# A hybrid decoder layer: PSUM tiles, ScalarE reads, gathered diagonal blocks, and two Z projections moved into the attention steps

## The chip, the cores and the metric

The kernel runs on one core of a Trainium2 chip. The metric is the device time of one execution in microseconds (us); several runs of a kernel are taken, and their median counts. The engines are TensorE (PE; its weight loads are listed as PEld), VectorE (DVE), ScalarE (ACT), GpSimd (POOL) and SyncE (SP, which here only issues DMAs). Each works through its own instructions in order.

## The reference, cut to what matters

One decoder layer on x of 1024 tokens by 1024 channels, float32:

```python
h = rmsnorm(x, attn_norm_w)
qkv_la, z_la, b_la, a_la, q_d, k_d, v_d = split(h @ w_in)
q, k, v = split(silu(causal_conv(qkv_la)))
o_la = rmsnorm(gated_delta_rule(q, k, v, g, beta)) * silu(z_la)
o_d = rmsnorm(diff_attention(q_d, k_d, v_d, lam, bias))
x = x + concat(o_la, o_d) @ w_out
gate, up = split(rmsnorm(x) @ w_gate_up)
x = x + (silu(gate) * up) @ w_down
return rmsnorm(x)
```

The delta rule works in chunks of 64 tokens and needs, per head and chunk, the solution of a unit lower triangular system. The attention has four heads with two softmax maps each, causal, in blocks of 128 queries. z_la has four heads of 128 columns; head h of it multiplies the normed output of the delta rule's head h and is needed nowhere before.

## The kernel before, in words

Every float32 matrix product is made of three matmuls (`mm3`, lines 143 to 146): both operands are split into a rounded part (`_h`) and a rest (`_l`), and h·h, h·l and l·h are added up in PSUM. `split` (148) makes the two parts of a weight: a cast on ScalarE (151), and a subtraction on VectorE (153) or, in two halves, on GpSimd (157). Projections keep the transposed input `xT_h`, `xT_l` in SBUF and take 48 matmuls of 512 columns per 128 output columns (8 slices of the depth, 2 halves of the tokens, 3 matmuls).

PSUM is used through three names: `big` (two tiles of two banks, 1024 columns), `sm` and `fl` (two tiles of one bank each). Instructions are put in order by a planner which goes by the program order, by what each one waits for, and by a cost of its own; only the SP queue is kept in the written order from the attention on (`manual_schedule`, 1024).

The stages in order:

- Norm and transposition of x, the projection of v_d and of the gates (to line 296), and small tables.
- Conv stage (463 to 486): for each of four heads the projections of k and q (`dense_T`, 415), the convolution and Silu, the sums of squares, and the products k·k and k·q, which give `At` (482, the triangular matrices, 128 x 128 each) and `intra` (485, in place in `dec`). Behind it two powers on GpSimd (489, 490) and the scaling of `rqs` on VectorE (491); rqs is used after the scan only (702).
- Triangular solve (498 to 515): the 32 x 32 diagonal blocks of all At are transposed into `B` by four transposes of 32 partitions each (504), inverted by 31 steps of two VectorE instructions (509, 511), and transposed back (514, 515). Meanwhile TensorE makes the attention's q and k projections of heads 0 and 1 (`qk_dense`, 517; called at 558) and two conv projections of v. `qk_dense` reads each half (512 columns) from PSUM twice for these heads: ScalarE writes the rounded part (535), VectorE the rest (536); then ScalarE's queue issues the stores (544, 545 for q, 547, 548 for k).
- The block inverses are put together (lines 585 to 624), the keys transposed (625), and the remaining v projections made.
- The scan over 8 chunk pairs (653 to 701), with Z projections between its small matmuls; then the rest of the four Z projections (709 to 713): a projection into a `big` tile, one Silu of 1024 columns on ScalarE, a store to `sz_dr`. The weights' rests come from VectorE.
- Attention: 32 steps (head, block of queries). `emit_S` (908) makes the scores, VectorE adds the bias and takes the maximum (932 to 938), ScalarE the exponential (942), `emit_P` VectorE's combination of the two maps (951 to 954), `emit_T` the transposition (969), `emit_PV` the product with V (984). Between these parts `pump` takes matmuls out of a generator `fill` (807): the q and k projections of heads 2 and 3, the gating of the delta rule's output (`finish_norm`, `finish_gate`, which loads sz_dr), and the output projection (`out_unit`, 787, with w_out's weights from `fetch_o`). `share` (886) says how many matmuls a step takes: 22 - 5i/2 for block i, less what other calls take. `fetch` (398) issues a weight load on SP, `take` (404) splits it. `load_head` (722) loads a head's q, k and bias.
- Norm and transposition again (to 1137), then 22 turns of gate and up (`gate_up`, 1215). A turn computes two products of 256 x 256 blocks of tokens and depth halves with seven block products instead of eight: `product` (1197), 12 matmuls each, seven per turn. `banks` (1203) gives four PSUM tiles: pa from `sm`, pb from `fl`, and pc and pd as the two halves of one `big` tile. VectorE's additions (`add`, 1213) read them. Turn 0 is written out (1289 to 1321).
- The down projection and the last norm (1350 to 1397).

## Time and profile before

| | us |
|---|---|
| three runs, median | 1364.12 (1363.31 to 1366.2) |
| the profiled execution's own time | 1363.61 |
| its span, first to last instruction | 1361.5 |
| mean granted TensorE clock | 0.99 of full speed |

The rows further down are lines of this one profiled execution. Times in them count from its first instruction. A line of a timeline or of the chain begins with the start and the duration in us. "L536" is line 536 of the kernel; "[6.28 <-DVE cv L536]" says that the engine stood idle for 6.28 us before, until VectorE's instruction of line 536 on tile cv was done. Names of tiles are those of the program, with buffer numbers left out, so `av` or `cv` stands for several arrays.

### The profile page before, as it was taken

To read this page: it belongs to the slowest core of one execution; us is meant where nothing else is said; L and a number is where in the kernel's file an instruction comes from. 1 tells how busy PE (TensorE), PEld (TensorE's weight loads), DVE (VectorE), ACT (ScalarE), POOL (GpSimd) and SP (SyncE) were. 2 spreads that over 40 slices of the span, in tenths; PEclk is the share of its full clock that TensorE was granted. 3 is DMA by queue.
4 is the path that set the end of the run, shared out by engine and by line. 5 is a ranking of instruction groups with operands and counts; after the bars stand their busy time and mean duration, and the time that the engine had idled before them with its cause. 6 is when DMAs were issued, how large, how long until landed. Compare 5 with 4: busy or idle time off the path is not lost.

```text
span 1361.5 us, 16980 instructions
## 1 busy us (share of the span) xinstructions
PE 1298.3 (95%) x6540; PEld 1078.0 (79%) x6540; DVE 766.1 (56%) x1286; ACT 484.7 (36%) x920; POOL 240.6 (18%) x195
## 2 busy tenths in 40 slices
PE   6999998899999998989889999999999999999997
PEld 6978886798988777877668777878787888888886
DVE  6515659634836675876875465545544546545325
ACT  5233321132725564654543332322332234112104
POOL 1010030200023331232321212121122114200003
PEclk9999998999999998999989999999999999999999
DMA  7321112301146466735322323222222147422003
GB/s 218 111 62 43 35 32 88 114 17 31 33 141 196 144 206 183 227 102 200 119 78 93 108 82 104 87 70 77 93 78 92 63 156 276 140 93 93 0 1 124
DMA packets 122424, 143.30 MB, mean 105 GB/s; under 512 B 13632, under 2 KB 90728, under 8 KB 122344
## 3 DMA queue, kind: packets, MB, share of 16 engines
q1 hardware_dynamic: 114432, 128.07, 30.1%
q10 hardware_dynamic: 7912, 14.16, 2.8%
q8 instruction: 51, 0.84, 0.2%
q14 instruction: 29, 0.24, 0.1%
HBM read 103.40 MB, written 38.80 MB: 104 GB/s over the span
## 4 chain that ended last, share of the span: by engine, by line
PE 72%; DVE 12%; DMA 5%; issue 4%; ACT 4%; POOL 2%; SPq 1%; POOLq 0%; DVEq 0%; ACTq 0%
PE big L1200 17%; PE sm L1200 8%; PE big L144 4%; PE big L146 4%; PE big L145 4%; PE fl L144 4%; PE fl L146 4%; PE fl L145 4%; PE fl L1200 4%; PE sm L144 3%; PE sm L145 3%; PE sm L146 3%; PE sm L984 1%; DVE tmp L509 1%; DVE av L511 1%
## 5 line engine op out<-in xcount | busy, mean ns | idle before, releaser
L144 PE MATMUL big<-xT_h,w_h 128*128 128x512 f32 x320 | 128.2, 401 | 10.7 <-DVE cv L536 10.0
L146 PE MATMUL big<-xT_h,w_l 128*128 128x512 f32 x320 | 126.5, 395 | 0.0
L145 PE MATMUL big<-xT_l,w_h 128*128 128x512 f32 x320 | 126.1, 394 | 0.0
L1213 DVE TENSOR_TENSOR av<-big,av 128x512 f32<-128x512 f32 x88 | 60.5, 689 | 107.9 <-PE big L1200 107.8
L1200 PE MATMUL big<-hT_h,cv 128*128 128x512 f32 x264 | 90.8, 405 | 2.3 <-DVE av L1213 2.3
L1200 PE MATMUL big<-hT_h,avl 128*128 128x512 f32 x264 | 89.3, 399 | 1.2 <-DVE av L1213 1.2
L144 PEld LDWEIGHTS big<-xT_h,w_h 128*128 128x128 f32 x320 | 60.6, 190 | 26.0 <-DVE cv L536 12.3
L151 ACT CAST w_h<-w_raw 128x1024 fp32r<-128x1024 f32 x32 | 33.5, 1052 | 124.6 <-PE big L145 103.2
L146 PEld LDWEIGHTS big<-xT_h,w_l 128*128 128x128 f32 x320 | 60.5, 189 | 13.1 <-DVE w_l L153 0.7
L145 PEld LDWEIGHTS big<-xT_l,w_h 128*128 128x128 f32 x320 | 60.6, 189 | 11.8 <-issue 0.2
L1200 PEld LDWEIGHTS big<-hT_h,cv 128*128 128x128 f32 x264 | 50.4, 191 | 20.2 <-DVE av L1213 9.8
L1200 PEld LDWEIGHTS big<-hT_h,avl 128*128 128x128 f32 x264 | 49.5, 188 | 18.3 <-DVE av L1213 8.1
L1200 PE MATMUL sm<-hB_h,avl 128*128 128x512 f32 x176 | 59.0, 397 | 1.1 <-ACT hB_h L1130 1.1
L157 POOL TENSOR_TENSOR w_l<-w_raw,w_h 128x512 fp32r<-128x512 f32 x28 | 37.8, 1371 | 124.5 <-ACT w_h L151 123.3
L1213 DVE TENSOR_TENSOR x<-fl,x 128x512 f32<-128x512 f32 x48 | 32.9, 686 | 46.1 <-PE fl L146 46.1
L1213 DVE TENSOR_TENSOR x<-sm,x 128x512 f32<-128x512 f32 x48 | 33.0, 687 | 44.9 <-PE sm L146 44.1
L1200 PE MATMUL sm<-hB_h,cv 128*128 128x512 f32 x176 | 57.9, 389 | 0.0
L1168 DVE TENSOR_TENSOR xh<-w_raw 128x512 f32<-128x512 f32 x45 | 31.0, 688 | 46.8 <-DMA w_raw<-in_w_gate_up 46.8
L942 ACT ACTIVATE ae<-big,mx 128x128 f32<-128x128 f32 (+7 forms) x64 | 47.3, 741 | 27.9 <-DVE mx L933 11.8
L1105 POOL TENSOR_TENSOR avl<-xh,avl 128x512 fp32r<-128x512 f32 x23 | 30.7, 1335 | 148.4 <-ACT avl L1104 148.4
L1105 POOL TENSOR_TENSOR cv<-xh,cv 128x512 fp32r<-128x512 f32 x22 | 28.4, 1289 | 146.7 <-ACT cv L1104 146.7
L1200 PE MATMUL big<-hT_l,cv 128*128 128x512 f32 x132 | 52.6, 398 | 0.0
(431 smaller groups left out, 3480.8 us busy)
## 6 DMA issues: line engine op xcount, KB each, us to landing
w_raw<-in_w_gate_up SPq DMA_DIRECT2D x44, 512.0 KB, 4.0
w_raw<-in_w_in SPq DMA_DIRECT2D x24, 512.0 KB, 4.0
act<-av SPq DMA_DIRECT2D x22, 512.0 KB, 2.6
w_raw<-act SPq DMA_DIRECT2D x22, 512.0 KB, 4.3
cv<-in_w_down SPq DMA_DIRECT2D x20, 512.0 KB, 4.0
xt<-in_x SPq DMA_DIRECT2D x8, 512.0 KB, 5.1
ks<-cv ACTq DMA_DIRECT2D x8, 512.0 KB, 13.7
aqh<-qh SPq DMA_DIRECT2D x16, 256.0 KB, 5.6
```

Source lines behind the costliest of these rows:

```text
L144: nc.tensor.matmul(ps, lhsT=lh, rhs=rh, start=start, stop=False)
L145: nc.tensor.matmul(ps, lhsT=lh, rhs=rl, start=False, stop=False)
L146: nc.tensor.matmul(ps, lhsT=ll, rhs=rh, start=False, stop=stop)
L151: nc.scalar.copy(out=h, in_=raw)
L157: eng.tensor_tensor(out=l[:, c], in0=raw[:, c], in1=h[:, c].bitcast(F32), op=ALU.subtract)
L509: nc.vector.tensor_tensor(out=tv, in0=B[:, i + 1:, i:i + 1].broadcast_to([P, nr, ncol]), in1=X[:, i:i + 1, :ncol].broadcast_to([P, nr, nco ...
L511: nc.vector.tensor_tensor(out=X[:, i + 1:, :ncol], in0=X[:, i + 1:, :ncol], in1=tv, op=ALU.subtract)
L942: nc.scalar.activation(out=e[:, :n].rearrange("p (b c) -> p b c", b=nb), in_=s[:, :, :w], func=AF.Exp, bias=mx[:, m:m + 1], accum_out=zs[: ...
L1105: eng.tensor_tensor(out=l, in0=raw, in1=h.bitcast(F32), op=ALU.subtract)
L1168: nc.vector.tensor_tensor(out=r, in0=a0, in1=a1, op=alu)
L1200: nc.tensor.matmul(ps, lhsT=x[:, k, :], rhs=y[:, k, :], start=begin and k == 0 and n == 0, stop=k == HALF - 1 and n == 2, skip_group_check ...
L1213: nc.vector.tensor_tensor(out=out, in0=in0, in1=in1, op=ALU.add)
```

## The change

Five edits:

1. `banks` takes two `big` tiles per turn and uses the first half of each; turn 0 keeps the two halves of one.
2. `qk_dense` of heads 0 and 1 reads PSUM with ScalarE twice, the second time as the full value into `sl`; VectorE subtracts the rounded part once for both halves, from SBUF.
3. In the conv stage ScalarE copies the diagonal blocks of each new At into an array `diag` (32 copies of 32 partitions x 4 x 32), and one transpose over 128 partitions makes `B`.
4. The scaling of rqs moves behind the assembly of the inverses.
5. Z projections 2 and 3 leave the loop behind the scan. They become the first part of `fill` (`z_dense`), with `fl` tiles, a Silu per half, and the weights' rests on GpSimd; their weights are fetched ahead of head 0's q and k, the weight loads for q and k of head 2 follow behind them, and the shares rise to 24.67 - 5i/2.

```diff
@@ -460,6 +460,7 @@
             nc.vector.tensor_reduce(out=dst[:, hh, half * 4:half * 4 + 4],
                                     in_=ps.rearrange("p (a b) -> p a b", a=4), axis=AX.X, op=ALU.add)
 
+    diag = op.tile([P, T], F32, name="av", bufs=4).rearrange("p (h c) -> p h c", c=32)
     for h in range(H):
         conv_silu(dense_T(C_K + h * P), 4 + h, KT[h])
         conv_silu(dense_T(C_Q + h * P), h, QT[h])
@@ -484,11 +485,13 @@
                                                op0=ALU.mult, op1=ALU.mult)
             nc.vector.tensor_tensor(out=dec[:, b0:b0 + 4, :], in0=kq.rearrange("p (a b) -> p a b", a=4),
                                     in1=dec[:, b0:b0 + 4, :], op=ALU.mult)
+            for q in range(4):
+                qs = slice(32 * q, 32 * q + 32)
+                nc.scalar.copy(out=diag[qs, b0:b0 + 4, :], in_=At[qs, b0:b0 + 4, qs])
     intra = dec
     fl = "p h t -> p (h t)"
     nc.gpsimd.tensor_tensor(out=nk.rearrange(fl), in0=ssk.rearrange(fl), in1=epow_pos, op=ALU.pow)
     nc.gpsimd.tensor_tensor(out=rqs.rearrange(fl), in0=ssq.rearrange(fl), in1=epow_neg, op=ALU.pow)
-    nc.vector.tensor_scalar(out=rqs, in0=rqs, scalar1=DK ** -0.5, scalar2=None, op0=ALU.mult)
     nc.vector.tensor_tensor(out=bup_f, in0=brk_f, in1=eGlG, op=ALU.mult)
 
 
@@ -499,9 +502,7 @@
     X = bx("X").rearrange("p (c s) -> p c s", s=32)
     nc.vector.memset(X, 0.0)
     nc.vector.memset(X.rearrange("p c s -> p (c s)")[:, 0::33], 1.0)
-    for q in range(4):
-        qs = slice(32 * q, 32 * q + 32)
-        nc.vector.transpose(out=B[qs], in_=At[qs, :, qs].rearrange("s h c -> s c h"))
+    nc.vector.transpose(out=B, in_=diag.rearrange("p h c -> p c h"))
     tmp = gp.tile([P, 256], F32, name="tmp", bufs=1)
     for i in range(31):
         nr, ncol = 31 - i, i + 1
@@ -533,8 +534,9 @@
             scale = DH ** -0.5 if is_q else 1.0
             if h < 2:
                 nc.scalar.mul(out=sh[:, ns], in_=ps, mul=scale)
-                nc.vector.scalar_tensor_tensor(out=sl[:, ns], in0=ps, scalar=scale, in1=sh[:, ns].bitcast(F32),
-                                               op0=ALU.mult, op1=ALU.subtract)
+                nc.scalar.mul(out=sl[:, ns].bitcast(F32), in_=ps, mul=scale)
+                if n == 1:
+                    nc.vector.tensor_tensor(out=sl, in0=sl.bitcast(F32), in1=sh.bitcast(F32), op=ALU.subtract)
                 continue
             nc.scalar.mul(out=sl[:, ns].bitcast(F32), in_=ps, mul=scale)
             nc.scalar.copy(out=sh[:, ns], in_=sl[:, ns].bitcast(F32))
@@ -622,6 +624,7 @@
                              start=True, stop=True)
         nc.vector.tensor_scalar(out=TT[h][0:64, :, 64:128], in0=ut[0:64].rearrange("p (j c) -> p j c", c=64),
                                 scalar1=-1.0, scalar2=None, op0=ALU.mult)
+    nc.vector.tensor_scalar(out=rqs, in0=rqs, scalar1=DK ** -0.5, scalar2=None, op0=ALU.mult)
     Ktok = gp.tile([P, NHJ, P], F32, name="ak", bufs=1)
     for h in range(H):
         Kh = Ktok[:, h * 8:h * 8 + 8, :]
@@ -706,7 +709,7 @@
     nc.gpsimd.tensor_tensor(out=oms, in0=oms, in1=epow_neg, op=ALU.pow)
     nc.vector.tensor_tensor(out=oms, in0=oms, in1=rq, op=ALU.mult)
 
-    for h in range(H):
+    for h in range(2):
         zps = dense_T(C_Z + h * P, nc.vector)
         sz = cvt()
         nc.scalar.activation(out=sz, in_=zps, func=AF.Silu)
@@ -804,8 +807,23 @@
         x2t[t] = op.tile([P, T], F32, name="avl", bufs=4)
         nc.sync.dma_start(out=x2t[t], in_=x2_dr[t])
 
+    def z_dense(h):
+        w = take(("z", h), nc.gpsimd)
+        fetch((2, h == 2), *qk_col(2, h == 2))
+        sz = cvt()
+        for n in range(2):
+            ps = flr()
+            ns = slice(n * 512, (n + 1) * 512)
+            for k in range(NK):
+                mm3(ps, w[0][:, k, :], w[1][:, k, :], xT_h[:, k, ns], xT_l[:, k, ns], k == 0, k == NK - 1)
+                yield 3
+            nc.scalar.activation(out=sz[:, ns], in_=ps, func=AF.Silu)
+        nc.scalar.dma_start(out=sz_dr[h], in_=sz)
+
     def fill():
         one = lambda n: flr()
+        yield from z_dense(2)
+        yield from z_dense(3)
         yield from qk_dense(2, True, one, lambda: finish_norm(0))
         fetch((3, True), *qk_col(3, True))
         finish_norm(1)
@@ -886,7 +904,7 @@
     def share(k):
         i = steps[k][1] if k < len(steps) else 0
         prev = steps[k - 1][1] if 0 < k <= len(steps) else 0
-        n = 22 - 5 * i / 2
+        n = 24.67 - 5 * i / 2
         pb = 4 if prev >= 4 else 0
         return max(0, n - pb - 5), pb, 5
 
@@ -1022,8 +1040,8 @@
             nc.scalar.dma_start(out=md[h][:, hc], in_=m)
 
     with tc.manual_schedule(engines={mybir.EngineType.SP}):
-        fetch((2, True), *qk_col(2, True))
-        fetch((2, False), *qk_col(2, False))
+        for h in (2, 3):
+            fetch(("z", h), w_in_v[:, :, C_Z + h * P:C_Z + (h + 1) * P], [P, NK, P])
         load_head(0)
         load_v(0)
         for k in range(len(steps) + 4):
@@ -1201,8 +1219,7 @@
                                  stop=k == HALF - 1 and n == 2, skip_group_check=not begin)
 
     def banks():
-        y = big()
-        return sma(), flr(), y[:, 0:512], y[:, 512:1024]
+        return sma(), flr(), big()[:, 0:512], big()[:, 0:512]
 
     def temps():
         return [op.tile([P, T], F32, name="av", bufs=4) for _ in range(3)]
@@ -1286,7 +1303,8 @@
         W0["A12"] = w_split(a12, nc.vector)
         W0["A22"] = w_split(a22, nc.vector)
 
-    pa, pb, pc, pd = banks()
+    pa, pb, both = sma(), flr(), big()
+    pc, pd = both[:, 0:512], both[:, 512:1024]
     tx, tg, tu = temps()
     u2, u3 = tx[:, n0], tx[:, n1]
     product(pc, W0["S3"], T3, True)
```

## Rows read from the trace of the kernel before

**Rows 1.** The page's busy times: us, share of the span, instructions.

```profile
PE 1298.3 (95%) x6540; PEld 1078.0 (79%) x6540; DVE 766.1 (56%) x1286; ACT 484.7 (36%) x920; POOL 240.6 (18%) x195
```

**Rows 2.** Windows by stage: start:end, length, busy us (count) of PE PEld DVE ACT POOL, clock, DMA share, GB/s.

```profile
186.00:271.00 85.00, 74.28 (x337) 59.77 (x335) 63.62 (x113) 16.22 (x22) 18.68 (x8) 0.96 0.27 86
388.00:410.00 22.00, 22.00 (x101) 18.30 (x100) 5.55 (x6) 4.19 (x6) 2.54 (x2) 1.00 0.80 235
410.00:446.00 36.00, 35.00 (x184) 28.98 (x182) 23.14 (x43) 21.08 (x48) 13.23 (x11) 1.00 0.62 185
...
508.00:521.00 13.00, 8.53 (x39) 7.35 (x38) 5.31 (x10) 5.50 (x14) 2.49 (x2) 0.74 0.51 179
...
600.00:620.00 20.00, 16.14 (x82) 13.29 (x81) 13.05 (x26) 9.43 (x25) 6.40 (x5) 0.91 0.49 172
```

**Rows 3.** Who PE waited for, whole span: us in total, times, longest.

```profile
PE big L144 <- DVE cv L536: 10.0, 4, 6.3
PE big L927 <- ACT ae L942: 6.7, 6, 4.4
PE sm L969 <- DVE ae L954: 6.4, 5, 3.8
```

**Rows 4.** VectorE's timeline, solve stretch.

```profile
203.46 0.18 DVE L491 TENSOR_SCALAR rqs<-rqs 128x32 f32<-128x32 f32 x1 [5.82 <-POOL rqs L490]
...
205.99 7.71 DVE L504 STREAM_TRANSPOSE av<-ak 32x1024 f32<-32x1024 f32 x4
213.73 0.69 DVE L536 SCALAR_TENSOR_TENSOR cv<-big,cv 128x512 fp32r<-128x512 f32 x1
...
214.45 1.22 DVE L153 TENSOR_TENSOR w_l<-w_raw,w_h 128x1024 fp32r<-128x1024 f32 x1
...
237.62 0.32 DVE L509 TENSOR_TENSOR tmp<-av 128x156 f32<-128x156 f32 x1
237.98 1.29 DVE L511 TENSOR_TENSOR av<-av,tmp 128x156 f32<-128x156 f32 x1
...
243.54 2.09 DVE L514 STREAM_TRANSPOSE av<-av 128x1024 f32<-128x1024 f32 x1
```

**Rows 5.** ScalarE's timeline, the same stretch.

```profile
204.43 0.59 ACT L535 ACTIVATE cv<-big 128x512 fp32r<-128x512 f32 x1
...
214.45 0.34 ACTq L545 DMA_DIRECT2D ql<-cv  x1
214.84 0.60 ACT L535 ACTIVATE cv<-big 128x512 fp32r<-128x512 f32 x1 [9.82 <-DVE tmp L509]
```

**Rows 6.** Window by instructions that read xT_h: PE PEld DVE ACT, clock, DMA share, GB/s.

```profile
214.40:218.40 4.00, 3.07 (x5) 1.45 (x5) 0.00 (x0) 0.00 (x0) 0.50 0.71 217
```

**Rows 7.** The chain that ended last, one turn of gate and up.

```profile
863.35 2.72 PE fl L1200 x12
...
869.69 2.93 PE big L1200 x12
...
878.07 2.97 PE big L1200 x12
...
882.85 2.72 PE fl L1200 x12
```

**Rows 8.** ScalarE's timeline, last Z readings and start of attention.

```profile
399.05 1.02 ACT L712 ACTIVATE cv<-big 128x1024 f32<-128x1024 f32 x1
...
409.93 1.02 ACT L712 ACTIVATE cv<-big 128x1024 f32<-128x1024 f32 x1
...
411.39 1.28 ACT L942 ACT_TABLE_LOAD   x1 [0.44 <-ACT cv L712]
```

**Rows 9.** The chain that ended last, attention, where the filler runs dry.

```profile
503.27 8.46 DMA w_raw<-in_w_out
```

**Rows 10.** The SP queue's timeline, head 0's first loads.

```profile
393.64 1.66 SPq L743 DMA_DIRECT2D aqh<-qh  x2
```

**Rows 11.** GpSimd's timeline, solve stretch.

```profile
237.69 2.70 POOL L157 TENSOR_TENSOR w_l<-w_raw,w_h 128x512 fp32r<-128x512 f32 x2 [34.26 <-ACT w_h L151]
```

## The prediction before the run

> **What bounds the kernel now.** I read the busy list first: TensorE is busy 1298.3 us of a span of 1361.5 us [rows 1], so what can be won is mostly time in which it stands still, or runs at the lower clock, and work taken away from it. Nothing in this change takes matmuls away; two projections only change place. So I looked for TensorE's idle time by stage, in the table of windows [rows 2]: the stretch from 186 to 271 us (the triangular solve beside the first attention projections) has 74.3 us busy of 85, the two dense Z projections from 388 to 410 us are full, the attention stretches have small holes and two larger ones (508 to 521 and 600 to 620 us). The list of waits says who ends them [rows 3]: 10.0 us for VectorE's line 536 in the solve stretch, the longest 6.3 us; 6.7 us for the exponentials (line 942) and 6.4 us for the combination of the two maps (line 954), both in attention.
>
> Why line 536 is late is in VectorE's timeline [rows 4]. It idles 5.82 us in front of line 491, a tiny scaling of rqs that waits for a power on GpSimd, although no one needs rqs before the end of the scan; then come four transposes of 32 partitions each, 7.71 us together, and only then line 536. ScalarE's timeline shows the second half of that knot [rows 5]: the store of the low part (line 545) is issued from ScalarE's queue, waits for line 536, and the next read of PSUM (line 535) stands behind it, 9.82 us late. TensorE waits 6.28 us of the 10.0 here and then runs at 0.50 of its clock, the 1.2 GHz level, for the 4.0 us from 214.4 to 218.4 us [rows 6]. At half rate these 4.0 us cost another 2.0 us. Loss of this stretch: 10.0 + 2.0 = 12.0 us.
>
> The gate and up loop (21 turns) is bound by TensorE with a pattern [rows 7]: from the start of one turn's product on fl to the next is 882.85 - 863.35 = 19.50 us. A product of 12 matmuls takes 2.72 us without a wait, seven products 19.04 us. The missing 0.46 us is in two of the seven, of 2.93 and 2.97 us: each of these writes one half of the big tile just after VectorE has read the other half.
>
> **The change part by part.**
>
> *Solve stretch (diagonal blocks, rqs, ScalarE reads).* Moving the rqs scaling takes 5.82 us of idle time out of VectorE's way. One transpose over 128 partitions takes the place of four over 32. An equal one over 128 x 1024 is in the trace at 2.09 us (line 514), so 7.71 - 2.09 = 5.6 us go. In return ScalarE makes 32 copies of 32 partitions x 128 columns; the nearest row copies 512 columns in 0.59 us (line 535), so one costs between almost nothing and 0.59 us. I take half, 0.3 us, as a quarter of the columns. 28 of them lie in the conv stage, where ScalarE has room; the last four, 1.2 us, stand between the last write of At and the transpose, beside line 485 on VectorE. VectorE's chain should thus begin and end some 10 us earlier. That by itself is worth nothing at the end, as TensorE has dense work up to 270.7 us; it is worth what TensorE waits for. Line 536 read PSUM on VectorE; now ScalarE reads twice (2 x 0.59 us) and VectorE subtracts once per projection from SBUF, 1024 columns, 1.22 us as line 153 shows, so 4 x 1.22 instead of 8 x 0.69 us. TensorE's big buffers come free without VectorE. What is queued behind: the store of the low part still waits for the subtract, on ScalarE's queue, with the next PSUM reads behind it, and the weights' low parts (line 153) are still made by VectorE inside the solve. So between 0 (the wait moves whole to the subtract) and 12.0 us come back; with VectorE no longer 13.5 us late I stand nearer the upper end and take three quarters: **-9.0 us**.
>
> *Separate banks.* With pc and pd in two tiles, neither of the two hand-offs has a reader to wait for. The buffers' reuse moves closer: pc of a turn must wait until the last addition of the turn before has read it, but two products (5.4 us) lie between, and the addition takes 0.69 us. Every hand-off that is gone gives 0.21 or 0.25 us: 21 x 0.46 = 9.7 us, at least 0 (if the order of products made for the old waits brings new ones). It is a plain count with the mechanism in the rows, so I take **-9.5 us**. Turn 0 keeps its old tiles.
>
> *Z projections 2 and 3.* Removed from the dense stretch: two times the distance of the Silu readings, 409.93 - 399.05 = 10.88 us [rows 8], 21.8 us. Added to the attention steps: 96 matmuls x 0.2267 us = 21.8 us, and the shares rise from 22 to 24.67 matmuls per step, 32 x 2.67 = 85 of the 96. TensorE's work is the same; only holes that are filled count. The attention waits are 6.7 + 6.4 = 13.1 us [rows 3]. The longest, 4.4 us at 514 us, comes with the point where the filler runs dry: ScalarE's cast of the w_out weights stands 8.46 us before its DMA [rows 9], with exponentials behind it. That point moves to other steps but stays; I count nothing for it, nor for its clock (0.74 over 13 us, 3.4 us [rows 2]). The other long one, 3.8 us at 611 us with 0.09 x 20 = 1.8 us of clock, is at the end, where the output units have run out; more filler lasts longer: half of 5.6, **-2.8 us** (0 to 5.6). The small ones are 13.1 - 4.4 - 3.8 = 4.9 us; 0.6 us more matmuls per step should cover most: **-3.0 us** (0 to 4.9).
>
> What the move adds: Silu and Exp don't share a table. The trace loads one between the last Silu and the first exponential, 1.28 us, 1.72 us from the Silu's end to the load's end [rows 8]. Four Silu calls between exponentials mean eight more loads, 8 x 1.28 = 10.2 us on ScalarE, all in the first four or five steps, where ScalarE is busy 21.1 of 36 us [rows 2]. They fit by sum, but a step's transposes wait for exponentials of the step before, so some show: between 0 and 8 x 1.72 = 13.8 us; I take **+3.0 us**, near the low end, because each load has a step of some 7 us to hide in. The Trainium skill ("ScalarE: Activation LUTs", section "What ACT_TABLE_LOAD costs") puts a switch at about 2.66 us, the 1283 ns load and a drain of 1380 ns; by it the eight would take 21.3 us of ScalarE. The load's own 1283 ns agrees with this trace; a drain of that length does not show between the two rows.
>
> Queues: the head's loads start at 393.64 us today [rows 10], behind a weight load that waits for its buffer. Now the two Z weights stand ahead of them, their buffers are free long before, and the scan's buffers (free at about 381 us) decide. Their landing must be covered by the one dense Z that is left over after the scan and by the fill; from nothing to 5 us uncovered: **+1.0 us**. The Z stores (two) go behind the Silu on ScalarE's queue as before. The splits of these weights go from VectorE to GpSimd, which is idle then, 2 x 1.3 us each. While GpSimd does such a split [rows 11], VectorE's line 511 took 1.29 us where its neighbour of the same size took 0.32 us [rows 4]: two splits can stretch VectorE by 2 x 1.9 us. The cover is Z matmuls in the scan; I take 0, with 3.8 as the end. The two 512 KB weight loads of the next projection only follow later on SP.
>
> **Sum:** -9.0 - 9.5 - 2.8 - 3.0 + 3.0 + 1.0 = -20.3 us on the profiled execution's own 1363.61 us: 1343.3 us. The runs' median is 0.5 us above that execution, so **1343.5 us**.
>
> **Rivals.**
> 1. *Everything fills* (chance 0.16). All 12.0 and 9.7 us return, and the end hole and the small waits close with no table load showing: -10.5. 1363.6 - 32.2 = 1331 us. For it: TensorE's holes are short. Against: the in-order queues of ScalarE and VectorE.
> 2. *The Z fill gives nothing* (0.17): loads show by 8 us and no hole closes. 1363.6 - 18.5 + 8 = 1353 us. For it: the shares were balanced to the steps.
> 3. *The separate tiles don't separate* (0.08): the planner's new order brings other waits of the same size in the loop. About 1353 us.
> 4. *Slower* (0.05): ScalarE becomes the bound of the first attention steps. Its place is the four Silu calls between exponentials: all eight loads on the path, 13.8 us, four stalls each followed by 4 us at 0.50 clock (2.0 us each as in [rows 6], 8.0 us), and the uncovered head load, 5 us: +26.8 against -18.5, 1372 us. It decides once more than 18.5 us of the move show. Against it: 15 us of ScalarE idle in those 36 us. The same page's section "Table sets: the hidden batching unit" asks for calls to be grouped by table, which this move undoes; by its 2.66 us a switch, all on the path, the time would be 1363.6 - 18.5 + 21.3 = 1366 us, and the 1.28 us row speaks for less.
>
> **How the numbers follow.** The forecast has 0.52, its own range 1336 to 1350. Rivals 1 to 3 reach from 1331 to 1353; with the bounds of the unknown terms the range is 1330 to 1357, which leaves out the slower case and the outermost ends. A difference under 0.2% (2.7 us) can't be told from none: faster than that 0.90 (forecast, rivals 1 to 3, less the overlap with the bound's end), within it 0.04, slower 0.06.
>
> **What would show it.** In the profile after: line 491's wait gone, one transpose of about 2 us, the list of waits without VectorE's subtract and no stretch of 0.50 clock between 208 and 219 us; seven products per turn in 19.0 to 19.1 us; eight or so table loads between the first exponentials and TensorE's waits for line 942 there. I am wrong if TensorE stands in the solve as long as before (a subtract or a weight split in front of it), if the turn stays at 19.5 us, or if the attention stretch grows by clearly more than 21.8 us.

## The result and the profile after

The changed kernel takes 1345.12 us (median of 4 runs, 1342.97 to 1345.69) against 1365.11 us before: ratio 0.9852, 95% interval 0.9835 to 0.9869, so 20 us faster. Timed again beside other runs of the kernel before, the ratio was 0.9849 (0.9824 to 0.9873). The forecast was 1343.5 us, the range 1330 to 1357 us. The profiled execution took 1345.63 us, 17.98 us less than the one before; its span is 1343.8 us, 17.7 us shorter. The rows below come from it.

Busy times of the page, to be read beside [rows 1]:

```profile
PE 1286.1 (96%) x6540; PEld 1079.8 (80%) x6540; DVE 759.3 (56%) x1277; ACT 505.6 (38%) x968; POOL 245.7 (18%) x199
```

TensorE has the same 6540 matmuls and is 12.2 us less busy: a matmul that waits for its tile, or runs at half rate, counts as busy for longer (in the gate and up loop, those into `big` from `cv` took 405 ns each before and take 389 ns now). ScalarE has 48 instructions and 20.9 us more: the 32 copies, eight more PSUM reads, six more table loads, and two more Silu calls, as Z is now read in halves.

The windows by stage (start:end, length, busy time and count of PE, PEld, DVE, ACT, POOL, clock, DMA share, GB/s), to be read beside [rows 2] and [rows 6]:

```profile
186.00:271.00 85.00, 77.80 (x365) 63.61 (x363) 61.20 (x108) 25.68 (x41) 21.45 (x10) 0.96 0.27 87
214.40:221.00 6.60, 5.11 (x12) 4.05 (x13) 6.05 (x17) 1.08 (x2) 0.00 (x0) 0.50 0.47 155
...
520.00:540.00 20.00, 14.34 (x76) 12.40 (x75) 12.11 (x26) 8.89 (x19) 3.50 (x3) 0.91 0.76 229
600.00:620.00 20.00, 19.62 (x96) 15.91 (x96) 8.49 (x20) 8.62 (x21) 6.47 (x6) 1.00 0.61 205
```

The solve stretch won 77.80 - 74.28 = 3.5 us of TensorE time, not 9, and still has a stretch at 0.50 clock, the 1.2 GHz level. It is no shorter than before: 6.6 us with TensorE busy 5.11 of them, where the kernel before has 0.50 from 212.50 to 219.20 us, busy 4.44 of 6.70 us. (The prediction's 4.0 us from 214.4 to 218.4 us are a part of that.) The attention's end (600 to 620 us) is full, at full clock. The hole of 508 to 521 us has moved to 520 to 540 us, and a new one lies at 465 to 480 us (TensorE busy 10.76 of 15 us, clock 0.89).

Whom TensorE waited for, in the solve and in attention (us in total, times, longest; the lines with the most), to be read beside [rows 3]:

```profile
PE sm L1002 <- ACT apt L988: 8.5, 2, 4.3
PE big L144 <- ACT cv L537: 3.9, 3, 1.9
PE big L146 <- DVE w_l L153: 2.7, 1, 2.7
...
PE sm L987 <- ACT apt L988: 2.0, 2, 1.6
PE big L945 <- ACT ae L960: 1.9, 2, 1.1
```

VectorE's subtract no longer stands here, as forecast; in its place come 3.9 us for ScalarE's read of PSUM and 2.7 us for a weight's low part. In attention the waits for the exponentials (line 960, before 942) and for the combination of the two maps (line 972, before 954) fall from 13.1 to 3.1 us, the 4.4 and 3.8 us ones among them; in their place come 10.5 us for ScalarE's copy of apt, with two long ones of 4.2 and 4.3 us.

VectorE's timeline of the solve, to be read beside [rows 4], shows why so little of the 9 us came:

```profile
204.47 0.18 DVE L627 TENSOR_SCALAR rqs<-rqs 128x32 f32<-128x32 f32 x1 [5.53 <-POOL rqs L494]
204.57 0.68 DVE L486 TENSOR_TENSOR dec<-sm,dec 128x512 f32<-128x512 f32 x1
...
207.57 2.09 DVE L505 STREAM_TRANSPOSE av<-av 128x1024 f32<-128x1024 f32 x1 [0.49 <-ACT av L490]
...
213.12 1.22 DVE L539 TENSOR_TENSOR cv<-cv 128x1024 fp32r<-128x1024 f32 x1
```

The scaling of rqs now stands 140 lines further down in the program (line 627), and yet the planner issues it in the same place as before, ahead of the last two writes of `dec`, and VectorE waits 5.53 us for the power on GpSimd as it did before (5.82 us [rows 4]). The second half of the edit did what it should: one transpose of 2.09 us for four of 7.71 us, and a subtract of 1.22 us.

ScalarE's timeline, to be read beside [rows 5]:

```profile
206.32 1.22 ACT L490 COPY av<-ak 32x128 f32<-32x128 f32 x4 [6.13 <-DVE ak L483]
...
214.37 0.34 ACTq L547 DMA_DIRECT2D ql<-cv  x1
214.75 0.60 ACT L536 ACTIVATE cv<-big 128x512 fp32r<-128x512 f32 x1 [5.16 <-DVE av L512]
```

The last four copies take 1.22 us, the price that the forecast had taken. The knot is the old one: the store of the low part waits for VectorE's subtract, and the next PSUM read behind it is 5.16 us late, where it was 9.82 us late.

A turn of gate and up in the chain that ended last, to be read beside [rows 7]:

```profile
850.20 2.72 PE fl L1218 x12
852.92 5.44 PE big L1218 x24
858.36 2.72 PE sm L1218 x12
861.08 5.44 PE big L1218 x24
866.52 2.72 PE sm L1218 x12
869.24 2.72 PE fl L1218 x12
```

869.24 - 850.20 = 19.04 us: seven products of 2.72 us, none longer. Both hand-offs are gone.

**Where the time went, stage by stage.** From the first rows of each stage in both traces: this execution began its conv stage 1.2 us later, ahead of any edit; over all runs here that start varies by 3.1 us. The first product of the block assembly (line 594, now 596) starts at 268.3 instead of 270.6 us: -3.5 us of the solve, net of that start. The first score matmul (line 927, now 945) starts 19.1 us earlier: 16.8 us more. These are two Z projections less (21.8 us), minus 22 fill matmuls of z_dense (5.0 us) that now run ahead of the first scores. The stretch from the first to the last score matmul grows by 14.2 us (196.8 to 211.0). From the last score matmul to the next transposes it is 0.8 us more, from there to the loop's first fl product 1.1 us less. The gate and up loop, from its first fl product to its last matmul, takes 409.5 instead of 424.4 us: -14.9. Behind it 2.3 us come back: 0.9 us are four matmuls of the down projection, which before ran inside the last turn, and 0.7 us a longer wait for line 1230 (1.38 instead of 0.69 us); the rest is spread thin.

### The profile page after: what moved, and what is told of

Same layout as the page of the kernel before. It is cut to its first block, busy times and chain, and to the rows that moved or that the text cites. A ratio compares the mean times of both kernels' runs of the same rounds, so it can differ in the third digit from the quotient of the medians.

```text
span 1343.8 us, 17054 instructions
## 1 busy us (share of the span) xinstructions
PE 1286.1 (96%) x6540; PEld 1079.8 (80%) x6540; DVE 759.3 (56%) x1277; ACT 505.6 (38%) x968; POOL 245.7 (18%) x199
## 4 chain that ended last, share of the span: by engine, by line
PE 41%; DVE 5%; DMA 3%; ACT 2%; issue 1%; POOL 1%; POOLq 0%; DVEq 0%; ACTq 0%; SPq 0%
PE big L1218 16%; PE sm L1218 8%; PE fl L1218 4%; PE fl L144 2%; PE fl L145 2%; PE fl L146 2%; PE sm L144 2%; PE sm L145 2%; PE sm L146 2%; DMA w_raw<-in_w_gate_up 1%; DMA w_raw<-act 1%; ACT cv L1397 1%; DMA cv<-in_w_down 1%; DVE x L1230 1%; DVE av L1230 1%
## 5 line engine op out<-in xcount | busy, mean ns | idle before, releaser
L144 PE MATMUL big<-xT_h,w_h 128*128 128x512 f32 x288 | 115.5, 402 | 4.5 <-ACT cv L537 3.9
L146 PE MATMUL big<-xT_h,w_l 128*128 128x512 f32 x288 | 114.3, 397 | 2.7 <-DVE w_l L153 2.7
L145 PE MATMUL big<-xT_l,w_h 128*128 128x512 f32 x288 | 113.9, 396 | 0.0
L1218 PE MATMUL big<-hT_h,cv 128*128 128x512 f32 x264 | 85.9, 389 | 0.0
L1218 PE MATMUL big<-hT_h,avl 128*128 128x512 f32 x264 | 85.8, 389 | 0.0
L157 POOL TENSOR_TENSOR w_l<-w_raw,w_h 128x512 fp32r<-128x512 f32 x32 | 43.1, 1369 | 202.2 <-ACT w_h L151 202.2
L144 PEld LDWEIGHTS big<-xT_h,w_h 128*128 128x128 f32 x288 | 54.8, 190 | 18.0 <-ACT cv L537 5.4
L146 PEld LDWEIGHTS big<-xT_h,w_l 128*128 128x128 f32 x288 | 54.7, 190 | 14.4 <-DVE w_l L153 3.1
L145 PEld LDWEIGHTS big<-xT_l,w_h 128*128 128x128 f32 x288 | 54.7, 190 | 10.8 <-issue 0.2
## 6 DMA issues: line engine op xcount, KB each, us to landing
ks<-cv ACTq DMA_DIRECT2D x8, 512.0 KB, 13.9
```

What stands on the lines that cost most here:

```text
L144: nc.tensor.matmul(ps, lhsT=lh, rhs=rh, start=start, stop=False)
L145: nc.tensor.matmul(ps, lhsT=lh, rhs=rl, start=False, stop=False)
L146: nc.tensor.matmul(ps, lhsT=ll, rhs=rh, start=False, stop=stop)
L157: eng.tensor_tensor(out=l[:, c], in0=raw[:, c], in1=h[:, c].bitcast(F32), op=ALU.subtract)
L1218: nc.tensor.matmul(ps, lhsT=x[:, k, :], rhs=y[:, k, :], start=begin and k == 0 and n == 0, stop=k == HALF - 1 and n == 2, skip_group_check ...
```

## The experiments

All ratios are to the kernel before on the same chip. Each is known to some 0.002 (2.7 us), so the difference of two to some 3.5 us. For the changed kernel 0.985 stands below, the middle of its two measurements.

**1. The banks alone undone** (e1_one_tile):

```
-        return sma(), flr(), big()[:, 0:512], big()[:, 0:512]
+        y = big()
+        return sma(), flr(), y[:, 0:512], y[:, 512:1024]
```

> The changed kernel with pc and pd put back as the two halves of one big tile; all else as changed. Theory A (the separate tiles carry most of the gain, by taking away both hand-off waits of every turn and the longer stalls behind them): the distance of two fl products is 19.50 us again instead of 19.04, and the kernel is 9.7 to 13 us slower than the changed one, so some 1355 to 1358 us. Rival (the loop's gain comes from elsewhere, such as an earlier start of the weight loads): under 5 us slower, below 1350 us. As predicted it would be 9.5 us slower.

Measured: 1360.98 us, ratio 0.9952 (0.9934 to 0.9970). That is 0.0102, 13.9 us, above the changed kernel, a little more than theory A's 9.7 to 13 us. (By the spans it is 1360.7 - 1343.8 = 16.9 us, but this trace has other low clock stretches besides.) The loop takes 424.1 us, as in the kernel before (424.4), and not 409.5. The chain that ended last, one turn of it:

```profile
861.15 2.72 PE fl L1218 x12
863.87 2.72 PE big L1218 x12
866.59 0.91 PE sm L1218 x4
867.50 2.90 PE big L1218 x12
...
875.83 2.97 PE big L1218 x12
...
880.61 1.59 PE fl L1218 x7
```

The two long products (2.90 and 2.97 us) are back and the turn is 880.61 - 861.15 = 19.46 us. The hand-off itself, in the trace of before (VectorE's addition, and the first weight load of the product of 2.93 us of [rows 7]):

```profile
868.83 0.69 DVE L1213 TENSOR_TENSOR av<-big,av 128x512 f32<-128x512 f32 x1 [1.05 <-PE big L1200]
869.57 0.19 PEld L1200 LDWEIGHTS big<-hT_h,cv 128*128 128x128 f32 x1 [0.30 <-DVE av L1213]
```

By the program (`gate_up`) this addition reads pc and the product writes pd. The two halves of one tile are two banks, and no byte of them is shared; still the product into one half waits for the reader of the other. In both kernels pc and pd are different banks; only whether they are one tile differs. So the wait belongs to the tile, and not to the bank.

That the loop won more than the 21 hand-offs is seen at its first turns: in the trace of before, TensorE waits 2.33 us for line 1213 at 710.43 us, in this run 2.48 us at 708.20 us, in the changed kernel 0.59 us. Behind the 2.33 us the clock is at 1.2 GHz (0.50 from 712 to 714 us, and 710.43 to 715.03 us for a product of 2.72 us), which the changed kernel doesn't have.

**2. The Z move alone undone** (e2_z_back): all four Z projections ahead of attention again, shares of 22, and the head's loads in the old order.

```
-    for h in range(2):
+    for h in range(H):
         zps = dense_T(C_Z + h * P, nc.vector)
...
-        yield from z_dense(2)
-        yield from z_dense(3)
```

> The changed kernel with all four Z projections behind the scan again and the shares at 22; all else as changed. Theory A (the move only fills some holes in attention and pays with new ones): 2 to 3 us slower than the changed kernel, some 1347 to 1348 us; TensorE's wait of 4.2 us at about 474 us is gone and the end hole back. Rival 1 (the move is a main part of the gain): 8 us or more slower. Rival 2 (it costs): the same or faster than the changed kernel.

Measured: 1349.12 us, ratio 0.9879 (0.9856 to 0.9902): 0.0029, 4.0 us, above the changed kernel; by the spans of the profiled executions 1345.7 - 1343.8 = 1.9 us. Whom TensorE waited for between 380 and 640 us:

```profile
PE sm L985 <- DVE ae L970: 6.5, 5, 3.8
PE big L943 <- ACT ae L958: 6.0, 6, 3.7
```

These are the waits of before [rows 3]. With the move 12.5 us become 3.1, and the waits for apt grow from 0.8 to 10.5 us. So the move's gain is small and at the edge of what the runs can tell.

**3. The solve edits alone undone** (e3_solve_back): the four transposes, VectorE's read of PSUM and the old place of the rqs scaling are back.

```
-    nc.vector.transpose(out=B, in_=diag.rearrange("p h c -> p c h"))
+    for q in range(4):
+        qs = slice(32 * q, 32 * q + 32)
+        nc.vector.transpose(out=B[qs], in_=At[qs, :, qs].rearrange("s h c -> s c h"))
...
-                nc.scalar.mul(out=sl[:, ns].bitcast(F32), in_=ps, mul=scale)
-                if n == 1:
-                    nc.vector.tensor_tensor(out=sl, in0=sl.bitcast(F32), in1=sh.bitcast(F32), op=ALU.subtract)
+                nc.vector.scalar_tensor_tensor(out=sl[:, ns], in0=ps, scalar=scale, in1=sh[:, ns].bitcast(F32),
+                                               op0=ALU.mult, op1=ALU.subtract)
```

> The changed kernel with the old solve: four transposes, line 536 on VectorE, no gathered blocks, the rqs scaling in its old place; separate tiles and the Z move stay. Theory A (the solve edits gave a third of what was forecast, as the planner put the rqs scaling back in front of VectorE's chain): 3 to 4 us slower than the changed kernel, some 1348 to 1349 us, with TensorE's waits for line 536 at 10 us again. Rival (they gave the 9 us of the forecast and something else took it back): 8 us or more slower.

Measured: 1350.71 us, ratio 0.9893 (0.9871 to 0.9915): 0.0043, 5.9 us, above the changed kernel; by the spans 1347.2 - 1343.8 = 3.4 us. TensorE's list of waits has its old first line again:

```profile
PE big L144 <- DVE cv L536: 10.0, 4, 6.3
```

From the first conv projection to the first block assembly product this run takes 198.8 us, as the kernel before (198.7); the changed kernel takes 195.2. The edits as made are thus worth 3.4 to 5.9 us, below the forecast's 9.

**4. The rqs scaling taken out of VectorE's way for good** (e4_rqs_folded): the factor goes into an instruction that is there anyway. As rqs is ssq to the power -1/2, multiplying ssq by 128 (DK) is the same as multiplying rqs by DK to the power -1/2.

```
-        nc.vector.tensor_scalar(out=ssq[:, hs], in0=ssq[:, hs], scalar1=1e-6, scalar2=None, op0=ALU.add)
+        nc.vector.tensor_scalar(out=ssq[:, hs], in0=ssq[:, hs], scalar1=1e-6, scalar2=float(DK), op0=ALU.add,
+                                op1=ALU.mult)
...
-    nc.vector.tensor_scalar(out=rqs, in0=rqs, scalar1=DK ** -0.5, scalar2=None, op0=ALU.mult)
```

> The changed kernel with the scaling of rqs folded into the addition that VectorE makes on the sum of squares anyway (add 1e-6, times 128, then the power), so that no VectorE instruction waits for GpSimd's power before the solve. Theory A (VectorE's 5.5 us of waiting there is what is left of the solve's knot, and the three waits of TensorE between 208 and 216 us, 4.7 us, with 2 us of clock behind them, hang on it): 4 to 6.5 us faster than the changed kernel, some 1339 to 1341 us. Rival (TensorE is held by ScalarE's queue, which stands behind the store, and by weights whatever VectorE does): the same as the changed kernel within 1.5 us.

Measured: 1338.54 us, ratio 0.9801 (0.9779 to 0.9823): 0.0049, 6.7 us, below the changed kernel, and clear of the kernel before. VectorE's timeline:

```profile
200.37 0.69 DVE L487 TENSOR_TENSOR dec<-sm,dec 128x512 f32<-128x512 f32 x1
201.55 2.09 DVE L506 STREAM_TRANSPOSE av<-av 128x1024 f32<-128x1024 f32 x1 [0.49 <-ACT av L491]
```

The windows of the solve stretch (columns as above):

```profile
200.00:208.00 8.00, 8.00 (x37) 6.61 (x36) 7.13 (x15) 3.21 (x7) 3.94 (x1) 1.00 0.17 68
208.00:216.00 8.00, 8.00 (x37) 6.44 (x36) 7.38 (x20) 1.59 (x3) 0.00 (x0) 1.00 0.43 131
```

The transpose begins at 201.55 instead of 207.57 us, TensorE is full from 200 to 216 us, and there is no stretch at the lower clock in the solve. The first block assembly product comes at 259.6 instead of 268.3 us, 8.1 us earlier net of a start that is 0.5 us earlier. So the forecast's mechanism was right, and its 9 us are there (3.5 + 8.1 = 11.6 us in this stretch, 3.4 + 6.7 = 10.1 us at the end), once the planner has no scaling left to put back.

**5. The same fold alone, in the kernel before** (e6_fold_alone). The edit is that of experiment 4.

> The kernel before with one edit: the factor of rqs is multiplied in where 1e-6 is added to ssq (as in the version with the folded factor), and VectorE's scaling of rqs is gone. Theory A (VectorE's 5.82 us wait on POOL's power alone starts the solve late, and TensorE's 6.28 us wait and the half clock behind it follow from that): 4 to 8 us faster than the kernel before, ratio 0.994 to 0.997, with the first of the four transposes near 201.5 us where it began at 205.1. Theory B (the four transposes of 7.71 us and VectorE's subtract behind ScalarE's store still end last): within 1.5 us of the kernel before, ratio 0.999 to 1.001.

Measured: 1360.65 us, ratio 0.9964 (0.9952 to 0.9977), 4.9 us faster, inside theory A's range. The solve stretch in windows and TensorE's first wait:

```profile
208.00:216.00 8.00, 5.28 (x21) 3.45 (x20) 7.49 (x21) 0.60 (x1) 0.00 (x0) 1.00 0.43 131
216.00:224.00 8.00, 8.00 (x37) 6.54 (x36) 7.55 (x18) 2.14 (x3) 0.00 (x0) 1.00 0.15 35
```

```profile
PE big L144 <- DVE cv L536: 5.9, 5, 1.7
```

The four transposes begin at 200.39 instead of 205.99 us. They still take 8.1 us and the waits on line 536 are still 5.9 us; but the longest is 1.7 instead of 6.3 us, and the clock stays at its upper level. The first block assembly product comes 193.1 us behind the first conv projection, where it was 198.7. Deleting one 0.18 us instruction of VectorE is worth 5 us by itself.

**6. No table switches** (e5_no_silu): the two Z fills are written out by a plain copy; this leaves the Silu of heads 2 and 3 out.

```
-            nc.scalar.activation(out=sz[:, ns], in_=ps, func=AF.Silu)
+            nc.scalar.copy(out=sz[:, ns], in_=ps)
```

> The changed kernel, with the two Z fills written out without their Silu (a plain copy in its place; this leaves out the Silu of Z heads 2 and 3), so that ScalarE needs no Silu table between the softmax's Exp. Theory A (the six extra table loads between 391 and 418 us are hidden: TensorE is busy 40.00 us of 40 there): same time as the changed kernel, ratio to the kernel before 0.983 to 0.987, with one table load left at the first Exp. Theory B (each 1.28 us load delays a softmax step that ends late somewhere further on): 3 to 8 us faster than the changed kernel, ratio 0.979 to 0.983.

Measured: 1347.75 us, ratio 0.9866 (0.9843 to 0.9890): no faster than the changed kernel. ScalarE's timeline of the changed kernel shows how a pair of loads sits between the steps:

```profile
404.75 1.28 ACT L820 ACT_TABLE_LOAD   x1
406.05 0.60 ACT L820 ACTIVATE cv<-fl 128x512 f32<-128x512 f32 x1
406.65 1.28 ACT L960 ACT_TABLE_LOAD   x1
407.95 0.69 ACT L960 ACTIVATE ae<-big,mx 128x512 f32<-128x512 f32 x1
```

It has seven loads between 391 and 418 us, where the kernel before has one; a load costs 1.28 us, and the next activation begins 0.01 to 0.02 us after it. From 389 to 420 us TensorE is busy 31.00 of 31 us in both runs, with ScalarE at 23.69 us here and 18.00 us in the run without Silu; from the first to the last score matmul this run isn't shorter (214.2 against 211.0 us). The switches are hidden, as far as some 3.5 us of doubt allow to tell.

**7. The Z move once more, on top of the fold** (e8_fold_z_back): the edits of experiments 2 and 4 together.

> The version with the folded factor, with all four Z projections back ahead of the attention steps. Theory A (the Z move closes the hole at the attention's end, about 3 us, and pays part of it back in ScalarE's waits on DMA): 1.5 to 4 us slower than the version with the folded factor, ratio 0.982 to 0.984. Theory B (the Z move gives nothing once the solve's stretch is full): within 1.5 us of it, ratio 0.979 to 0.981.

Measured: 1339.17 us, ratio 0.9815 (0.9793 to 0.9837), 0.0014 or 1.9 us above the version with the fold, by the medians 0.6 us. Both theories' ranges (0.982 to 0.984 and 0.979 to 0.981) miss it by 0.0005. The two long waits of before are back (4.60 us for an exponential at 502.85 us; 3.83 us for line 970 at the attention's end, with a clock of 0.86 from 600 to 620 us), the long ones for apt are gone. Experiments 2 and 7 together put the move at 1 to 4 us; that it gives anything on top of the fold is not shown.

**8. The new holes in attention: four tries at them**, all on the version with the fold. Of the two waits for apt, the trace of the changed kernel gives the causes in ScalarE's timeline:

```profile
473.14 0.62 ACT L542 CAST cv<-cv 128x512 fp32r<-128x512 f32 x1 [4.89 <-DMA ks<-cv]
473.66 0.58 ACT L988 COPY apt<-sm 128x512 f32<-128x512 f32 x1
...
523.73 1.04 ACT L151 CAST w_h<-w_raw 128x1024 fp32r<-128x1024 f32 x1 [4.71 <-DMA w_raw<-in_w_out]
524.68 0.47 ACT L988 COPY apt<-sm 128x384 f32<-128x384 f32 x1
```

A cast stands at the head of ScalarE's queue and waits for a DMA (a store that must leave the buffer, a weight load that must land), and the copy of apt, for which TensorE waits, is behind it. The first try asks for the first w_out split two fill turns later (e7_late_take):

```
+        for _ in range(2):
+            yield -1
         w = [take_o(0, 0, nc.vector)]
...
-        for _ in range(SKIP):
+        for _ in range(SKIP - 2):
             yield -1
```

> The version with the folded factor, with the first two splits of w_out's weights asked for two fill turns later, so that their load has landed before ScalarE's cast stands at the head of its queue. Theory A (ScalarE, blocked 4.33 us at 515 us by the load of w_raw, is what starves TensorE there): the 4.2 us wait of TensorE for apt near 517 us goes and the time falls by 2 to 5 us against the version with the folded factor, ratio to the kernel before 0.976 to 0.979. Theory B (the wait is made up for by the rest of the attention steps, or moves to the next load): within 1.5 us of that version, ratio 0.979 to 0.981.

Measured: 1338.50 us, ratio 0.9802 (0.9783 to 0.9820), as the version with the fold. But the wait that it was to remove is still there: a cast of w_raw at 516.24 us waits 4.95 us (in the version with the fold 4.33 us, at 515.47 us). The casts of the first pair wait for nothing now (2.15 and 0.75 us there). It is the second pair that blocks: its take moved by two turns as well, but its loads stand behind the first take and moved with it. So neither theory was put to the test. The next moves the second take behind the four skipped turns (e9_second_take_late):

```
-        w.append(take_o(0, 1, nc.gpsimd))
-        fetch_o(1, 0, 0)
-        fetch_o(1, 0, 1)
         for _ in range(SKIP):
             yield -1
+        w.append(take_o(0, 1, nc.gpsimd))
+        fetch_o(1, 0, 0)
+        fetch_o(1, 0, 1)
```

> The version with the folded factor, with the second pair of splits of w_out's weights (the one whose cast stood 4.33 us at the head of ScalarE's queue at 515 us) asked for after the four skipped turns instead of ahead of them, and the two loads behind it with it. Theory A (that blocked head starves TensorE): the 4.33 us wait of ScalarE and TensorE's 4.2 us wait for apt near 517 us go, and the time falls by 2 to 5 us against the version with the folded factor, ratio to the kernel before 0.976 to 0.979. Theory B (the wait is made up for further on in the attention steps, or the later loads of w_out are now late in their turn): within 1.5 us of that version, ratio 0.979 to 0.981.

Measured: 1342.27 us, ratio 0.9811 (0.9783 to 0.9840); the changed kernel beside it on this chip 0.9849. A cast still waits, 4.93 us at 517.88 us, right ahead of the copy of apt, where it stood before: the planner keeps it early, and again neither theory was put to the test. Only at the fourth output unit, far behind (e11_take_at_unit3), is the head of the queue nearly free:

```
+            if n == 3:
+                w.append(take_o(0, 1, nc.gpsimd))
+                fetch_o(1, 0, 0)
+                fetch_o(1, 0, 1)
```

> The version with the folded factor, with the second pair of splits of w_out's weights asked for at the fourth unit of the output projection (its weights are needed from the ninth on), the loads behind it with it. Theory A (ScalarE's blocked head starves TensorE): no cast of w_raw waits over 1 us for a DMA between 505 and 530 us, TensorE's 4.2 us wait for apt goes, and the time falls by 2 to 5 us against the version with the folded factor, ratio 0.976 to 0.979. Theory B (the four skipped fill turns leave TensorE without other work between 512 and 525 us, so each step's own chain shows there whatever ScalarE waits for): within 1.5 us, ratio 0.979 to 0.982.

Measured: 1340.69 us, ratio 0.9809 (0.9782 to 0.9836). ScalarE's casts and TensorE's waits:

```profile
509.06 1.05 ACT L151 CAST w_h<-w_raw 128x1024 fp32r<-128x1024 f32 x1 [2.22 <-DMA w_raw<-in_w_out]
513.93 1.06 ACT L151 CAST w_h<-w_raw 128x1024 fp32r<-128x1024 f32 x1
519.49 1.04 ACT L151 CAST w_h<-w_raw 128x1024 fp32r<-128x1024 f32 x1
```

```profile
PE sm L1003 <- ACT apt L989: 4.2, 1, 4.2
PE fl L144 <- DVE xh L796: 4.1, 1, 4.1
```

Two of the three casts wait for nothing now and one waits 2.22 us; the wait for apt that is left, 4.2 us, ends at 470.04 us, in another step. In its place TensorE waits 4.1 us at 524.81 us for VectorE's addition of the output units (line 796). The ratio lies in theory B's range. That doesn't settle it, because this trace, and that of the last run beside it on the same chip, has a stretch at the 1.2 GHz level that no other trace has there:

```profile
268.30:278.50 10.20, 10.20 (x52) 8.82 (x52) 0.83 (x2) 2.88 (x5) 0.00 (x0) 0.50 0.00 0
```

From the first block assembly product to the first score matmul this run takes 126.3 us, the version with the fold 121.6. From the first score matmul to the transposes behind attention this run takes 242.4 us, the version with the fold 244.9; but traces with the same attention (experiments 1, 3 and 4, the changed kernel) range from 243.2 to 245.5. So a gain of some 2 us is neither shown nor excluded. The last run is the same with two skipped turns for four (e12_unit3_two_skips: SKIP = 2).

> The run beside it with two skipped fill turns instead of four, so that the output projection's first units come earlier into the steps. Theory A (the blocked head): no further gain over the run beside it, within 1.5 us of it. Theory B (the empty turns): TensorE has fill matmuls of w_out between 512 and 520 us, and the time falls by 2 to 5 us against the run beside it, unless the first split is then late itself (a wait of TensorE for w_l or w_h above 2 us), in which case it stays.

Measured: 1337.28 us, ratio 0.9791 (0.9771 to 0.9812). Its profiled execution, 1343.31 us, is the slowest of its five: there fill matmuls run to 515.3 us, a cast waits 4.29 us again, and TensorE waits 4.9 us for an exponential. Against the run beside it the ratio is 0.0018 (2.5 us) lower, in theory B's range but within the doubt. By medians it is the fastest kernel of all, but its interval overlaps those of experiment 4 and of the other tries; that it is faster than the fold is not shown. What would close these holes stays open.

The changed kernel itself was run again on the chip of e9_second_take_late (e10_changed_again):

> The changed kernel itself, for a comparison on the chip of the run beside it. Both theories: ratio to the kernel before 0.983 to 0.987, 6 to 8 us above the version with the folded factor.

Measured: 1346.11 us, ratio 0.9849 (0.9824 to 0.9873).

**What to keep:** the change together with the fold of experiment 4, 1338.54 us, beats both kernels.

## Why the prediction was right, and which terms were off

The total came out at -17.98 us on the profiled execution (forecast -20.3). All three parts gave something, by the mechanisms that the forecast names; but that the total came so near is partly luck. The solve gave some 5.5 us less than its term and the separate tiles some 4.5 us more, and the two errors cancel; the Z move came out near its sum with terms that didn't hold one by one. (1343.3 + 0.5 is 1343.8 and not 1343.5, which changes nothing.) Term by term:

- **Solve edits: -9.0 forecast, -3.4 to -5.9 measured.** The step that failed here is "Moving the rqs scaling takes 5.82 us of idle time out of VectorE's way". The order of VectorE's work is the planner's and not the program's, which the text before the prediction says; the planner put the moved instruction back to where it had been, and the 5.53 us wait stayed. The pieces of this term held: the transposes (5.6 us less), the four copies (1.2 us), the subtract (1.22 us), the knot with the store. ("No longer 13.5 us late" took more than the pieces give: 5.82 + 5.6 - 1.2 is some 10 us.) Experiment 4 shows the rest of the term when the instruction is truly gone. So the forecast "no stretch of 0.50 clock" was wrong for the changed kernel and right for that version.
- **Separate banks: -9.5 forecast, some -14 measured** (13.9 by experiment 1; the loop is 14.9 us shorter, of which 0.9 are the four matmuls that now run behind it). The count was right where it was made: from the second turn's fl product to the last turn's, the 19 turns take 362.6 instead of 372.6 us, 19 x 0.46 = 8.7 us and 1.3 us from one turn that was held up 2.1 us before. What was left out is that stalls outside the steady turn end on the same hand-off: up to the second turn's product 3.6 us more go (1.7 of the 2.33 us wait on line 1213, and the half rate behind it), and 1.4 us behind the last one, the four matmuls among them. The forecast read one regular turn and multiplied.
- **Z move: -1.8 forecast, -1 to -4 measured, but of other parts.** By the stages above it is -16.8 + 14.2 + 0.8 = -1.8 us. The end hole, which I took at half, closed (3.8 us and the clock), and 1.66 us for line 796 came at 623.83 us. The table loads, +3.0, cost nothing: seven and not nine, each in a step where TensorE has other work (experiment 6). The page "ScalarE: Activation LUTs" of the Trainium skill, section "What ACT_TABLE_LOAD costs", puts a switch at about 2.66 us with a drain in it. The rows here differ: the load is 1.28 us, and the switch no more than that and 0.02 us. The head's load, +1.0, cost nothing: it starts at 378.61 us, 15 us earlier than before [rows 10], and the fill covers it. The small waits, -3.0, went only from 4.9 to 3.1 us. The 4.4 us wait behind ScalarE's cast of w_out moved and stayed, as forecast (4.3 us at 525.20 us); the 8.46 us of [rows 9] are the load's duration, and ScalarE stood idle for 4.53 us of it in front of the cast. What the forecast put at nothing is a second place of that mechanism: at 474.29 us TensorE waits 4.2 us behind a cast that waits for a store, and then runs at the 1.2 GHz level (0.89 clock from 465 to 480 us).

Of the rivals, "the Z fill gives nothing" is nearest to the truth of its part by its result, and not by its reason: the loads don't show, and holes closed while others opened. "Everything fills" (1331 us) fell on the solve and on the waits for apt; "the tiles don't separate" and "slower by table loads" are excluded by experiments 1 and 6. The parts undone one by one add up to 13.9 + 4.0 + 5.9 = 23.8 us against 20.5 for the whole; with some 3.5 us of doubt on each that is no contradiction.

## What to carry to other kernels

To take an instruction off a path in a kernel whose order a planner makes, delete it (fold its factor into a neighbour) rather than move its line, and look in the trace for whether it moved. Where a steady pattern of small waits comes from one tile that is written and read in halves, give it two tiles; and look beside the pattern for irregular stalls that end on the same hand-off. Fill work for one engine that needs another engine's in-order queue (here a cast behind a DMA) closes one hole and can open the next.

## What was not expected of the hardware

- A load of ScalarE's table is followed by its activation within 0.02 us, and six more of them within 27 us left no trace in the time (ratio 0.9866 without them, 0.985 with them).
- TensorE's clock in the solve: before, TensorE stood 6.28 us up to 214.47 us, and the granted clock was 0.50 (1.2 GHz) from 212.50 to 219.20 us. In the changed kernel it stood 0.36, 2.66 and 1.63 us up to 215.89 us, and the clock was 0.50 from 214.40 to 221.00 us. With 0.88, 0.51 and 1.33 us in experiment 5 the clock stays at 1.00 (2.4 GHz) from 208 to 224 us. So 4.1 us less of waiting for line 536 than before (10.0 to 5.9) also ended the half rate, which had cost half of 4.44 us.
- The clock also fell with TensorE full: in e11_take_at_unit3 TensorE was busy 8.00 of 8 us from 260 to 268 us at 1.00, and then 10.20 of 10.20 us at 0.50. Why is open.
- GpSimd's power on 128 x 32 elements takes 5.44 us (two in a row, at 193.60 and 199.00 us), and VectorE's instruction of 0.18 us behind it waits for all of it, 5.53 us.
